# Casts of a projection's weights placed behind the sigmoids and evictions of the stage before, and two buffers for the latents

## The chip, the core and the metric

The kernel runs on one NeuronCore of a Trainium2 chip. Its engines work side by side, each through its own queue of instructions in order: TensorE (PE in the profile, with PEld for its weight loads), VectorE (DVE), ScalarE (ACT), GpSimd (POOL) and SyncE (SP), which here issues every DMA. An instruction that waits holds up all that stands behind it on its engine. The metric is the time of one execution on the device in microseconds (us), as the median of several runs.

## The reference, cut to what matters

A trunk of two layers over 512 tokens of width 1024. Layer 0 mixes with neighbourhood attention, layer 1 with latent attention; after each mixer comes a gated per-layer embedding.

```python
for i in range(DEPTH):
    xn = rmsnorm(x, norm_g[i])
    y = mixer_na(xn, ...) if i % 2 == 0 else mixer_mla(xn, ...)
    h = x + y
    gate = sigmoid(rmsnorm(h, ple_norm[i]) @ ple_w_gate[i])
    x = h + gate * (p[i] @ ple_w_proj[i])

# mixer_mla, its start:
c_q, c_kv, k_rope, z = split(xn @ w_in, [384, 640, 672], axis=-1)
q  = rmsnorm(c_q, q_norm) @ w_qb        # 16 heads of 64 + 32 (rotary)
kv = rmsnorm(c_kv, kv_norm) @ w_kvb
```

The change lies where layer 0 ends (its gate) and layer 1 begins: the projection to the latents `c_q`, `c_kv`, `k_rope` (672 columns), and the branch `z` (1024 columns).

## The kernel before

Tokens stand in four tiles of 128 rows (`t` = 0 to 3), and 1024 rows of weights in eight blocks `k`. A product of fp32 accuracy is made of three matmuls, high by high, low by high and high by low. Each weight matrix is therefore loaded raw and split by a cast: ACT writes the high part, DVE or POOL subtracts to get the low one. For the gate the parts are in fp32r (tiles `whi`, `wlo`, made by `load_w`); for layer 1's input projection in fp16 (tiles `whl`, and one `whx`), after a scaling by a power of two (`sc`) that depends on the sum of squares of the whole matrix.

**The end of layer 0, `gate_phase`.** The 1024 output columns go in two halves, `n` = 0 and 1; in each half four products of 24 matmuls, one for each `t`, go into two PSUM banks (`ps_mm`) in turn. A bank comes free when ACT has put its sigmoid (`sg`, line 692) into SBUF; DVE multiplies it with the embedding `pe` (line 693) and adds it to the residual `r` (line 695). After `n` = 1 of each `t`, `done` forms `x1n`, the normed input of layer 1 (square on ACT, a power on POOL, a product on DVE, lines 237 to 244), PE turns it in eight transposes, and ACT and DVE write it as fp16 parts `x1h`, `x1l` (lines 196, 197).

**The weights of the latents, `mla_ahead`.** They are prepared while the gate runs, in steps that `gate_phase` calls after given (`n`, `t`). `mla_c0` and `mla_c1` lie in two tiles `cr` (384 columns of `k` = 0..3 and 4..7, and two blocks of 288), `mla_c2` and `mla_c3` (three blocks of 288 each) in two of the three raw buffers `wraw`, through which the gate's own weights pass as well. ACT squares all of them (line 635); `over_rows` sums on PE; `scale` forms `sc` and its inverse `un`; four steps `cast` make the fp16 weights of the 384 columns (`c_cast`, lines 672 and 673, two halves of 384 elements a step). Steps `fetch` load the weights of `z`.

**The start of layer 1, `mla_c`.** Part 0 makes 384 columns for each `t`, part 1 the other 288. ACT evicts them (line 721) into tiles `c`. During part 0 the code casts the weights of part 1 (`whl`, `whl`, `whx`) and squares those of `z`; then `value_scale` (lines 203 to 218) loads the value weights `wv` and squares them. Last, for each `t`, the latents are normed into a tile `cn` (lines 237 to 244, 746 to 754), turned in six transposes and split into `cT` and into the rows `slab` of the rotary key, which SP moves to where the heads want them (line 191). There is one buffer for `cn`. `mla_heads` runs six products of the branch `z` (`NEARLY`, 24 matmuls each), then the rotary part, queries and keys of the first heads (line 784), two more products of `z`, and the heads.

**What sets the order.** The program is not written in the order that runs. A scheduler of the framework places the instructions of each engine by priority and by what its own model expects to be ready; `issue_after` (and `behind`, several of them) tells it to place what is inside no sooner than behind a given instruction. The built order is fixed; only semaphore waits decide the times. Tiles of a pool take over the place of a tile that has been released, and wait for its readers.

Of the kernel before, what the change touches and what calls it, by code (L numbers as in the profile page):

```python
# [14 lines left out]
F32 = mybir.dt.float32  # L15
# [4 lines left out]
AF = mybir.ActivationFunctionType  # L20
# [3 lines left out]
P = 128  # L24
S = 512
# [7 lines left out]
UP = 32768.0  # L33
# [12 lines left out]
class Trunk:  # L46
# [573 lines left out]
    def mla_ahead(self, junk, xinv):  # L620

        nc, a = self.nc, self.a
        raw = [self.big.tile([P, 1824], F32, name="cr", tag="big") for i in range(2)]
        raw += [self.wp.tile([P, 1024], F32, name="wraw", tag="wraw", bufs=3)[:, :864] for i in range(2)]
        ss = [self.small.tile([P, 8], F32, name="wss", tag="wss", bufs=4)[:, :4] for i in range(2)]
        self.c_raw, self.c_w, self.z_raw, self.z_sq = raw, [], [], []

        zj = [self.zp.tile([P, S], F32, name="z", tag="z") for i in range(2)]

        def load():  # L630
            for r, w in zip(raw, a["mla_c"]):
                nc.sync.dma_start(r, w)

        def square(r, c, k, i):
            nc.scalar.activation(junk[:, :c.stop - c.start], raw[r][:, c], AF.Square, accum_out=ss[k][:, i:i + 1])

        def squares(r):
            if r < 2:
                for i in range(2):
                    square(r, slice(768 * i, 768 * i + 768), 0, 2 * r + i)  # L640
                square(r, slice(1536, 1824), 1, r)
            else:
                square(r, slice(0, 864), 1, r)

        def scale():
            s = self.power(self.over_rows(ss), UP ** -2)
            u = self.small.tile([P, 8], F32, name="un", tag="un", bufs=8)[:, :2]
            nc.vector.reciprocal(u, s)
            nc.vector.tensor_scalar(u, u, xinv, None, op0=ALU.mult)
            self.c_scale = [(s[:, i:i + 1], u[:, i:i + 1]) for i in range(2)]  # L650

        def cast(q):
            h = self.pair16()
            self.c_cast(h, 0, raw[q // 2][:, q % 2 * 768:(q % 2 + 1) * 768], 0, 384)
            self.c_cast(h, 384, raw[q // 2][:, q % 2 * 768:(q % 2 + 1) * 768], 384, 384)
            self.c_w.append(h)

        def fetch(i):
            f, sq = self.fetch16([a["mla_z"][2 * i], a["mla_z"][2 * i + 1]], by="dve" if i in (2, 3) else "act",
                                 junk=zj[i // 2].bitcast(BF16))  # L660
            self.z_raw.append(f)
            self.z_sq += sq

        P_ = partial
        return {(0, 0): [load, P_(squares, 0)], (0, 1): [P_(squares, 1)], (0, 2): [P_(squares, 2), P_(squares, 3)],
                (0, 3): [scale], (1, 0): [P_(cast, 0), P_(cast, 1), P_(fetch, 0)], (1, 1): [P_(cast, 2), P_(cast, 3), P_(fetch, 1)],
                (1, 2): [P_(fetch, 2)], (1, 3): [P_(fetch, 3)]}

    def c_cast(self, h, o, r, c, w, part=0):
        nc = self.nc  # L670
# [4 lines left out]
    def gate_phase(self, pool, layer, hnT, rh, res, after, steps):  # L675
        nc, a = self.nc, self.a
        for n in range(2):
# [3 lines left out]
            for t in range(NT):  # L681
# [3 lines left out]
                w = S // 2 if last else S  # L685
                for o in range(0, S, w):
                    ps = self.psum("mm")[:, :w]
                    L = lambda s, k: hnT[t][:, s * KD + k, :]
                    W = lambda s, k: ws[k // 2][s][:, (k % 2) * S + o:(k % 2) * S + o + w]
                    self.mms(ps, self.by_chunk(L, W))  # L690
                    sg = pool.tile([P, S], F32, name="sg", tag="sg", bufs=2)[:, :w]
                    nc.scalar.activation(sg, ps, AF.Sigmoid, scale=rh[t])  # L692
                    nc.vector.tensor_tensor(out=sg, in0=pe[:, o:o + w], in1=sg, op=ALU.mult)  # L693
                    r = res[t][:, n * S + o:n * S + o + w]
                    nc.vector.tensor_tensor(out=r, in0=r, in1=sg, op=ALU.add)
                    after(t, n, o, w)
# [4 lines left out]
    def mla_c(self, pool, xT, cT, sets, xinv):  # L701
        nc, a = self.nc, self.a
# [9 lines left out]
        for part, (w0, wn) in enumerate(((0, 384), (384, 288))):  # L712
            un = self.c_scale[part][1]
            for t in range(NT):
# [3 lines left out]
                else:  # L718
                    W = lambda s, k: self.c_w[k // 2][:, s, (k % 2) * 384:(k % 2 + 1) * 384]
                self.mms(ps[:, :wn], self.by_chunk(lambda s, k: L(xT[s], k, t), W))  # L720
                nc.scalar.activation(cs[t][:, w0:w0 + wn], ps[:, :wn], AF.Copy, scale=un)
                if part == 0 and t < 3:
                    h = self.pair16() if t < 2 else pool.tile([P, 2, 1024], F16, name="whx", bufs=1)
                    if t == 0:
                        for i in range(2):
                            self.c_cast(h, 288 * i, self.c_raw[i], 1536, 288, 1)
                    else:
                        self.c_cast(h, 0, self.c_raw[1 + t], 0, 432, 1)
                        self.c_cast(h, 432, self.c_raw[1 + t], 432, 432, 1)
                    w1.append(h)  # L730
                if part == 0:
                    for i in range(2):
# [4 lines left out]
        slab_l = pool.tile([P, S], F32R, name="slab_l", tag="slab", bufs=2)  # L737
        for t in range(NT):
            c = cs[t]
            cn = pool.tile([P, 768], F32, name="cn", tag="cn", bufs=1)  # L740
            self.rms(cn[:, 0:384], c[:, 0:384], gq, 384)
            self.rms(cn[:, 384:640], c[:, 384:640], gkv, 256)
            cos, sin = tok[:, t, 0, :], tok[:, t, 1, :]
# [531 lines left out]
```

## Time and profile before

| | |
|---|---|
| median of 3 runs | 661.76 us (661.69 to 662.82) |
| the profiled execution: its own time | 659.6 us |
| its span, first to last instruction | 657.8 us |
| TensorE clock granted, mean of the span | 0.996 |
| matmuls | 3737 |
| moved by DMA | 80.2 MB, 122 GB/s on average |

The profiled execution is one run, 2.2 us under the median; its time holds 1.8 us outside the span. In what follows, columns of the table of windows are: the stretch and its length in us, then for each engine busy us and number of instructions, then the granted TensorE clock, the share of DMA engines busy, and GB/s. Rows of the timeline are: start, length (us), engine, line, operation, out<-in, shape, count; in brackets the idle time before it on that engine and what ended it.

### The profile page before, as it was taken

The numbers are of one execution on the slowest core, as the hardware profiler recorded it, in microseconds if no ns is written. First come the engines' busy times: TensorE is split into PE (matmuls) and PEld (weight loads), VectorE is DVE, ScalarE is ACT, GpSimd is POOL, SyncE is SP. The second block draws the span as 40 slices with busy tenths as digits, with TensorE's granted clock in tenths as the row PEclk, the third lists the DMA queues.
The fourth block names the chain that finished last, engine by engine and source line by source line (L and its number), as shares of the span: only waits on it lengthen the run. The fifth ranks groups of instructions, "written<-read, shape, count | busy, mean of one in ns | idle before, by whom it ended". The sixth has DMA issues, their size and how long they took to land.

```text
span 657.8 us, 10705 instructions
## 1 busy us (share of the span) xinstructions
PE 641.7 (98%) x3737; PEld 471.7 (72%) x3737; DVE 415.4 (63%) x955; ACT 435.3 (66%) x942; POOL 292.2 (44%) x295
## 2 busy tenths in 40 slices
PE   8999999999999999998999999999999999999995
PEld 6876575766856778886766454877777877788885
DVE  6387986867757316647767335888888874134543
ACT  6789977976757743655668445888878887245333
POOL 0341232342427575332102221686959776672721
PEclk9999999999999999999999999999999999999998
DMA  8957132400104055621860024120302222961122
GB/s 279 413 204 295 65 105 77 183 24 1 37 13 145 28 197 222 244 97 64 300 240 18 13 72 108 40 77 25 81 18 69 60 97 78 352 224 67 65 80 96
DMA packets 32327, 80.20 MB, mean 122 GB/s; under 512 B 4497, under 2 KB 9361, under 8 KB 32273
## 3 DMA queue, kind: packets, MB, share of 16 engines
q1 hardware_dynamic: 32272, 79.52, 34.4%
q8 instruction: 29, 0.48, 0.3%
q14 instruction: 26, 0.21, 0.1%
HBM read 67.97 MB, written 8.39 MB: 116 GB/s over the span
## 4 chain that ended last, share of the span: by engine, by line
PE 68%; ACT 11%; DVE 10%; DMA 4%; issue 4%; SPq 2%; POOL 1%; POOLq 0%; DVEq 0%; ACTq 0%
PE ps_mm L226 35%; PE ps_S L226 11%; PE ps_mm L784 5%; PE ps_T L255 5%; PE ps_T L226 3%; PE ps_O L226 2%; PE ps_O L898 2%; ACT whl L164 2%; DMA wraw<-gate 2%; PE ps_T L553 1%; PE ps_O L454 1%; ACT ex L878 1%; DMA wraw<-na_z 1%; ACT junk L137 1%; SPq L191 1%
## 5 line engine op out<-in xcount | busy, mean ns | idle before, releaser
L89 POOL TENSOR_TENSOR wlo<-wraw,whi 128x1024 fp32r<-128x1024 f32 (+3 forms) x63 | 109.5, 1759 | 67.0 <-ACT whi L88 34.0
L226 PEld LDWEIGHTS <-whl 128*128 128x128 f16 x648 | 62.3, 98 | 71.4 <-issue 1.3
L880 POOL TENSOR_TENSOR ex<-ex,rc 128x512 f32<-128x512 f32 x64 | 66.1, 1043 | 32.4 <-DVE rc L879 23.2
L88 ACT ACTIVATE whi<-wraw 128x1024 fp32r<-128x1024 f32 (+3 forms) x65 | 50.9, 812 | 43.0 <-DMA wraw<-gate 17.8
L226 PE MATMUL ps_mm<-whi,hnT 128*128 128x512 f32 (+1 forms) x272 | 70.2, 379 | 2.6 <-ACT sg L692 2.6
L226 PE MATMUL ps_mm<-xh,whl 128*128 128x512 f16 x304 | 72.6, 379 | 0.0
L197 DVE SCALAR_TENSOR_TENSOR pt<-ps_T,pt 128x512 f16<-128x512 f32 (+1 forms) x96 | 62.5, 661 | 15.6 <-ACT pt L196 15.3
L196 ACT ACTIVATE pt<-ps_T 128x512 f16<-128x512 f32 (+1 forms) x96 | 53.5, 575 | 9.3 <-PE ps_T L553 5.4
L226 PEld LDWEIGHTS ps_mm<-whi,hnT 128*128 128x128 f32 x272 | 49.2, 188 | 12.1 <-ACT sg L692 3.0
L540 POOL TENSOR_TENSOR ex<-ex,rc 128x128 f32<-128x128 f32 (+1 forms) x64 | 34.4, 569 | 50.5 <-DVE rc L536 42.2
L876 DVE TENSOR_REDUCE mx<-ps_S 128x1 f32<-128x512 f32 x64 | 43.7, 688 | 10.4 <-PE ps_S L226 9.1
L878 ACT ACTIVATE ex<-ps_S,mx 128x512 f32<-128x512 f32 x64 | 43.8, 685 | 9.7 <-DVE mx L876 8.8
L165 DVE SCALAR_TENSOR_TENSOR whl<-wr,sc,whl 128x512 f16<-128x512 f32 x64 | 45.6, 762 | 4.1 <-ACT whl L164 3.9
L239 POOL TENSOR_TENSOR rs<-ss,half 128x1 f32<-128x1 f32 x20 | 11.4, 576 | 76.3 <-DVE ss L238 76.2
L164 ACT ACTIVATE whl<-wr,sc 128x512 f16<-128x512 f32 x64 | 41.1, 712 | 4.4 <-DVE sc L100 2.6
L226 PE MATMUL ps_mm<-wlo,hnT 128*128 128x512 f32 (+1 forms) x136 | 40.6, 379 | 0.0
L255 PE MATMUL ps_T<-ident,ex 128*128 128x128 f32 x256 | 38.5, 273 | 0.0
L99 POOL TENSOR_TENSOR sc<-sc,half 128x1 f32<-128x1 f32 (+2 forms) x15 | 10.7, 713 | 62.2 <-DVE sc L98 62.2
L693 DVE TENSOR_TENSOR sg<-pe,sg 128x512 f32<-128x512 f32 (+1 forms) x17 | 21.6, 1270 | 24.7 <-ACT sg L692 24.7
L255 PEld LDWEIGHTS ps_T<-ident,ex 128*128 128x128 f32 x256 | 31.2, 140 | 8.2 <-POOL ex L880 1.1
L226 PE MATMUL ps_mm<-xl,whl 128*128 128x512 f16 x152 | 36.2, 379 | 0.0
L226 PE MATMUL ps_mm<-whl,xh 128*128 128x256 f16 x224 | 30.9, 273 | 0.6 <-DVE vt L197 0.3
(376 smaller groups left out, 1526.2 us busy)
## 6 DMA issues: line engine op xcount, KB each, us to landing
wr<-na_qk SPq DMA_DIRECT2D x16, 512.0 KB, 5.7
wraw<-gate SPq DMA_DIRECT2D x16, 512.0 KB, 3.3
pe<-pe SPq DMA_DIRECT2D x24, 256.0 KB, 7.0
wr<-na_v SPq DMA_DIRECT2D x8, 512.0 KB, 7.1
wraw<-na_o SPq DMA_DIRECT2D x8, 512.0 KB, 4.1
wr<-mla_z SPq DMA_DIRECT2D x8, 512.0 KB, 9.7
wraw<-mla_o SPq DMA_DIRECT2D x8, 512.0 KB, 4.9
wraw<-na_z SPq DMA_DIRECT2D x6, 512.0 KB, 7.8
```

What stands on the lines that cost most here:

```text
L88: nc.scalar.activation(hi[:, c], raw[:, c], AF.Copy)
L89: (rest or nc.gpsimd).tensor_tensor(out=lo[:, c], in0=raw[:, c], in1=hi[:, c].bitcast(F32), op=ALU.subtract)
L164: self.cast = [nc.scalar.activation(h[:, 0, c], r[:, c], AF.Copy, scale=s), nc.vector.scalar_tensor_tensor(h[:, 1, c], r[:, c], s, h[:, 0, ...
L165: nc.vector.scalar_tensor_tensor(h[:, 1, c], r[:, c], s, h[:, 0, c], op0=ALU.mult, op1=ALU.subtract)]
L196: self.last_split = nc.scalar.activation(hi, src, AF.Copy, scale=scale)
L197: nc.vector.scalar_tensor_tensor(lo, src, scale, hi, op0=ALU.mult, op1=ALU.subtract)
L226: last = self.last_mm = nc.tensor.matmul(out, l, r, start=i == 0, stop=i == n - 1)
L255: self.last_mm = self.nc.tensor.transpose(t[:, i * P:(i + 1) * P], b, self.ident)
L540: nc.gpsimd.tensor_tensor(out=e, in0=e, in1=rc[:, qt:qt + 1].to_broadcast([P, e.shape[1]]), op=ALU.mult)
L876: nc.vector.reduce_max(mx, sp, axis=AX.X, negate=True)
L878: nc.scalar.activation(ex, sp, AF.Exp, bias=mx, accum_out=sm)
L880: nc.gpsimd.tensor_tensor(out=ex, in0=ex, in1=rc.to_broadcast([P, S]), op=ALU.mult)
```

## The change

Four things are changed.

1. The four steps `cast` move: one after (1, 0), two after (1, 1), one after (1, 2), where two stood after (1, 0) and two after (1, 1); and each is placed behind the last sigmoid (`self.last_sg`). The casts for part 1 are placed behind the eviction of part 0 for the same `t`.
2. `mla_c2` and `mla_c3` are loaded in four pieces of 432 columns into buffers of the pool `zp`, which hold the branches' outputs `z`, instead of into two of the three `wraw`. Their squares and sums are six numbers in place of four.
3. The power in `scale` gets the priority that `scale16` has.
4. `cn` has two buffers.

```diff
-        raw += [self.wp.tile([P, 1024], F32, name="wraw", tag="wraw", bufs=3)[:, :864] for i in range(2)]
-        ss = [self.small.tile([P, 8], F32, name="wss", tag="wss", bufs=4)[:, :4] for i in range(2)]
+        raw += [self.zp.tile([P, S], F32, name="z", tag="z")[:, :432] for i in range(4)]
+        ss = [self.small.tile([P, 8], F32, name="wss", tag="wss", bufs=4)[:, :n] for n in (4, 6)]
...
-            for r, w in zip(raw, a["mla_c"]):
+            for r, w in zip(raw, a["mla_c"][:2] + [w[:, c:c + 432] for w in a["mla_c"][2:] for c in (0, 432)]):
                 nc.sync.dma_start(r, w)
...
-                square(r, slice(0, 864), 1, r)
+                square(r, slice(0, 432), 1, r)
...
         def scale():
-            s = self.power(self.over_rows(ss), UP ** -2)
+            ps = self.over_rows(ss)
+            with self.tc.high_priority(offset=300):
+                s = self.power(ps, UP ** -2)
...
         def cast(q):
             h = self.pair16()
-            self.c_cast(h, 0, raw[q // 2][:, q % 2 * 768:(q % 2 + 1) * 768], 0, 384)
-            self.c_cast(h, 384, raw[q // 2][:, q % 2 * 768:(q % 2 + 1) * 768], 384, 384)
+            with self.behind(self.last_sg):
+                for i in range(2):
+                    self.c_cast(h, 384 * i, raw[q // 2][:, q % 2 * 768:(q % 2 + 1) * 768], 384 * i, 384)
...
-        return {(0, 0): [load, P_(squares, 0)], (0, 1): [P_(squares, 1)], (0, 2): [P_(squares, 2), P_(squares, 3)],
-                (0, 3): [scale], (1, 0): [P_(cast, 0), P_(cast, 1), P_(fetch, 0)], (1, 1): [P_(cast, 2), P_(cast, 3), P_(fetch, 1)],
-                (1, 2): [P_(fetch, 2)], (1, 3): [P_(fetch, 3)]}
+        return {(0, 0): [load, P_(squares, 0)], (0, 1): [P_(squares, 1)], (0, 2): [P_(squares, 2 + i) for i in range(4)],
+                (0, 3): [scale], (1, 0): [P_(cast, 0), P_(fetch, 0)], (1, 1): [P_(cast, 1), P_(cast, 2), P_(fetch, 1)],
+                (1, 2): [P_(cast, 3), P_(fetch, 2)], (1, 3): [P_(fetch, 3)]}
...
-                    nc.scalar.activation(sg, ps, AF.Sigmoid, scale=rh[t])
+                    self.last_sg = nc.scalar.activation(sg, ps, AF.Sigmoid, scale=rh[t])
...
-                nc.scalar.activation(cs[t][:, w0:w0 + wn], ps[:, :wn], AF.Copy, scale=un)
+                ev = nc.scalar.activation(cs[t][:, w0:w0 + wn], ps[:, :wn], AF.Copy, scale=un)
                 if part == 0 and t < 3:
+                  with self.behind(ev):
...
-            cn = pool.tile([P, 768], F32, name="cn", tag="cn", bufs=1)
+            cn = pool.tile([P, 768], F32, name="cn", tag="cn", bufs=2)
```

Since the scheduler sets the order, three places of the built programs follow. The first is ACT in the second half of the gate, from the last sigmoid before the casts on (`sg` are the sigmoids, `whl<-cr` the casts, `x1n` the squares for the norm). Before:

```order
L692 ACTIVATE sg<-ps_mm,rs 128x512
L672 ACTIVATE whl<-cr,sc 128x384 x8
L672 ACTIVATE whl<-cr,sc 128x288 x2
L672 ACTIVATE whl<-wraw,sc 128x432 x2
L692 ACTIVATE sg<-ps_mm,rs 128x512 x2
L237 ACTIVATE x1n,ss<-r 128x1024 x2
```

In the changed program the same stretch of ACT reads:

```order
L695 ACTIVATE sg<-ps_mm,rs 128x512 x4
L675 ACTIVATE whl<-cr,sc 128x384 x2
L237 ACTIVATE x1n,ss<-r 128x1024
L695 ACTIVATE sg<-ps_mm,rs 128x512
L675 ACTIVATE whl<-cr,sc 128x384 x4
L237 ACTIVATE x1n,ss<-r 128x1024
L196 ACTIVATE x1h<-ps_T,sc 128x4x128 x2
L695 ACTIVATE sg<-ps_mm,rs 128x512
L675 ACTIVATE whl<-cr,sc 128x384 x2
```

Twelve casts stood in one piece ahead of the sigmoids of `t` = 0 and 1; now eight stand behind three of them, and the four of part 1 have gone to the stage after it, behind its evictions.

The second place is ACT at the end of the six early products of `z` (`z<-ps_mm` evicts one of them, `cT` and `slab_h` split the turned latents; the last `slab_h` belongs to `t` = 3; `ke` to `qo` evict the first heads' keys and queries, `rh` their rotary part). Before:

```order
L290 ACTIVATE z<-ps_mm,un 128x512
L88 ACTIVATE whi<-wraw 128x384 x2
L290 ACTIVATE z<-ps_mm,un 128x512
L176 ACTIVATE cT_3857<-ps_T 128x4x128
L176 ACTIVATE cT_3857<-ps_T 128x128
L176 ACTIVATE slab_h<-ps_T 128x128
L164 ACTIVATE whl<-wr_3849,sc 128x512 x4
L176 ACTIVATE ke_3863<-ps_S 64x512
L176 ACTIVATE ko_3865<-ps_S 64x512
L176 ACTIVATE qe_3859<-ps_S 64x512
L176 ACTIVATE qo_3861<-ps_S 64x512
L816 ACTIVATE rh<-ps_mm 128x512
```

And in the changed program:

```order
L176 ACTIVATE cT_3865<-ps_T 128x4x128
L176 ACTIVATE cT_3865<-ps_T 128x128
L176 ACTIVATE slab_h<-ps_T 128x128
L290 ACTIVATE z<-ps_mm,un 128x512
L88 ACTIVATE whi<-wraw 128x384 x2
L290 ACTIVATE z<-ps_mm,un 128x512
L164 ACTIVATE whl<-wr_3857,sc 128x512 x2
L820 ACTIVATE rh<-ps_mm 128x512
L164 ACTIVATE whl<-wr_3857,sc 128x512 x2
L176 ACTIVATE ke_3871<-ps_S 64x512
```

The last splits of the latents moved ahead of the last two evictions of `z`, and the eviction of the rotary part ahead of those of the keys and queries. On PE the six transposes of `t` = 3 stood behind all 144 matmuls of the six products; now 42 of these stand behind them.

The third place is SP from the last weights of `z` (`wr<-mla_z`) to the first move of `slab`. Before:

```order
L128 DMA wr_3849<-mla_z 128x1024 x2
L204 DMA wv<-mla_kv 128x4x512
L87 DMA wraw<-mla_qr 128x192 x2
L87 DMA wraw<-mla_kv 128x512
L1135 DMA spill_84<-r 128x1024
L87 DMA wraw<-mla_kv 128x512
L203 DMA gcol<-kv_norm 128x2x1
```

And in the changed program, from the same weights of `z` on:

```order
L128 DMA wr_3857<-mla_z 128x1024 x2
L87 DMA wraw<-mla_qr 128x192 x2
L87 DMA wraw<-mla_kv 128x512 x2
L87 DMA wraw<-mla_qn 128x384 x2
L1139 DMA spill_84<-r 128x1024
L203 DMA gcol<-kv_norm 128x2x1
L707 DMA tok<-rope_tok 128x128
L248 DMA gq<-q_norm 128x384
L248 DMA gkv<-kv_norm 128x256
L204 DMA wv<-mla_kv 128x4x512
L87 DMA wraw<-mla_qr 128x192 x2
```

The load of `wv` moved behind eleven other issues. In the changed program its tile takes the place of the first `cr`, and the issue waits for DVE's cast of the 288 columns from it, which is now in `mla_c`; before, it waited for PE alone.

More of the change, by code (lines that the diff above doesn't have):

```diff
@@ L727, in mla_c @@
                     else:
-                        self.c_cast(h, 0, self.c_raw[1 + t], 0, 432, 1)
-                        self.c_cast(h, 432, self.c_raw[1 + t], 432, 432, 1)
+                        for i in range(2):
+                            self.c_cast(h, 432 * i, self.c_raw[2 * t + i], 0, 432, 1)
                     w1.append(h)
```

## The prediction

> **What bounds the kernel.** I read the page's head first: TensorE is busy for 98% of the span, so a gain has to be idle time of PE.
>
> ```profile
> span 657.8 us, 10705 instructions
> PE 641.7 (98%) x3737; PEld 471.7 (72%) x3737; DVE 415.4 (63%) x955; ACT 435.3 (66%) x942; POOL 292.2 (44%) x295
> ```
>
> Second, the table of windows over the stages that the change touches (first column after the length: PE).
>
> ```profile
> 250.00:305.00 55.00, 55.00 (x267) 45.52 (x266) 32.76 (x38) 27.72 (x48) 22.70 (x13) 1.00 0.45 159
> 305.00:315.00 10.00, 7.45 (x33) 5.83 (x32) 9.60 (x21) 8.03 (x15) 0.59 (x1) 1.00 0.14 38
> 330.00:340.00 10.00, 10.00 (x70) 6.93 (x69) 8.64 (x13) 4.90 (x12) 0.55 (x1) 1.00 0.93 336
> 340.00:350.00 10.00, 9.85 (x81) 7.21 (x80) 2.64 (x10) 6.95 (x15) 1.25 (x3) 1.00 0.13 41
> 380.00:390.00 10.00, 9.39 (x50) 4.98 (x49) 3.04 (x14) 4.59 (x13) 2.55 (x5) 1.00 0.12 39
> 400.00:410.00 10.00, 8.62 (x38) 4.33 (x37) 4.40 (x8) 4.60 (x9) 1.15 (x2) 1.00 0.33 98
> 420.00:640.00 220.00, 219.62 (x1218) 173.29 (x1218) 144.10 (x272) 146.26 (x303) 149.66 (x122) 1.00 0.29 97
> ```
>
> PE lacks nothing up to 305, 2.55 us in the second half of the gate, 0.15 at 340 to 350 (I take that as staying), 0.61 at the end of the six early `z` products, 1.38 around the first score. From 420 to 640 it lacks 0.38 in 220 us, so whatever PE gains ahead of that passes to the end. Third, PE's timeline at these gaps, with the releaser in brackets.
>
> ```profile
> 287.80 1.07 PE L226 MATMUL ps_mm<-whi,hnT 128*128 128x512 f32 x4
> 298.89 1.17 PE L226 MATMUL ps_mm<-whi,hnT 128*128 128x512 f32 x4
> 312.60 1.19 PE L226 MATMUL ps_mm<-whi,hnT 128*128 128x512 f32 x4 [2.56 <-ACT sg L692]
> 314.10 1.07 PE L226 MATMUL ps_mm<-whi,hnT 128*128 128x512 f32 x4
> 315.46 1.07 PE L226 MATMUL ps_mm<-whi,hnT 128*128 128x512 f32 x4
> 348.65 0.28 PE L211 MATMUL ps_T<-half,vss 128*128 128x1 f32 x2
> 357.35 1.89 PE L226 MATMUL ps_mm<-x1l,whl 128*128 128x512 f16 x8
> 359.07 3.62 PE L226 MATMUL ps_mm<-x1h,whl 128*128 128x512 f16 x16
> 388.34 0.82 PE L255 MATMUL ps_T<-ident,cn 128*128 128x128 f32 x6
> 389.77 0.98 PE L784 MATMUL ps_mm<-cT,whi 128*128 128x512 f32 x3 [0.61 <-ACT cT L176]
> 401.51 1.89 PE L226 MATMUL ps_mm<-x1h,whl 128*128 128x512 f16 x8 [0.78 <-ACT z L290]
> 407.00 0.70 PE L226 MATMUL ps_S<-ke,qe 96*128 96x512 f32 x2
> 408.16 0.47 PE L226 MATMUL ps_S<-ke,qe 96*128 96x512 f32 x1 [0.45 <-DMA qe<-rl]
> ```
>
> Fourth, ACT's timeline ahead of the first gap.
>
> ```profile
> 285.28 1.06 ACT L88 ACTIVATE whi<-wraw 128x1024 fp32r<-128x1024 f32 x1 [0.37 <-DMA wraw<-gate]
> 286.25 0.67 ACT L692 ACTIVATE sg<-ps_mm,rs 128x512 f32<-128x512 f32 x1
> 305.87 5.01 ACT L672 ACTIVATE whl<-cr,sc 128x384 f16<-128x384 f32 x10 [3.63 <-DVE sc L100]
> 311.88 1.25 ACT L692 ACTIVATE sg<-ps_mm,rs 128x512 f32<-128x512 f32 x2
> ```
>
> **Part 1, casts behind sigmoids: −2.55.** The second half of the gate starts on PE at 298.89. From 314.10 to 315.46 six matmuls take 1.36, 0.227 each, so `t` = 0 is done 24 × 0.227 = 5.4 later, at 304.3. Its sigmoid comes only at 311.88, behind ten casts (row at 305.87) and two more that follow them; they waited for `sc` until 305.87 and took 6.0. PE wants that bank for `t` = 2 after 48 matmuls, at 309.8, and waits 2.56. In the new order of ACT no cast is ahead of the sigmoid of `t` = 0: it runs at 304.3 to 305.0, 4.8 before the bank is wanted, and that of `t` = 1 at 309.8 is wanted at 315.2. At most two casts, 1.0 us, stand ahead of it. The gap goes; the bound is 0 to 2.55.
>
> What is late next are the casts and splits themselves, now between the norms. The chain from the sigmoid of `t` = 0 to its norm's end took from 311.88 to 317.53, the end of the first row below: 5.65. Further rows are the sums of squares of `z`'s weights, and two groups of DVE from 300 to 350 (total, and mean in ns).
>
> ```profile
> 316.25 1.28 DVE L244 SCALAR_TENSOR_TENSOR x1n<-r,rs,gn 128x1024 f32<-128x1024 f32 x1 [0.66 <-POOL rs L239]
> 334.06 1.22 DVE L133 CUSTOM_DVE_ANT_0 z<-wr 128x1024 bf16<-128x1024 f32 x1
> ...
> L693 DVE TENSOR_TENSOR sg<-pe,sg 128x512 f32<-128x512 f32 x5 | 5.5, 1100 | 3.0 <-ACT sg L692 3.0
> L695 DVE TENSOR_TENSOR r<-r,sg 128x512 f32<-128x512 f32 x5 | 3.5, 691 | 0.1
> L197 DVE SCALAR_TENSOR_TENSOR x1l<-ps_T,sc,x1h 128x512 f16<-128x512 f32 x8 | 5.8, 747 | 3.0 <-ACT x1h L196 3.0
> ```
>
> From 304.3 that gives 309.9, or 310.9 with two casts on ACT ahead; the built order of PE places these transposes after some 70 of the half's 96 matmuls, at 298.9 + 70 × 0.227 = 314.8. Slack 3.9. The tightest is the low part of `t` = 3 on DVE. From the end of that sigmoid, about 325.6, DVE has its product and sum, four sums of squares, a norm, and four low parts: 1.10 + 0.69 + 4 × 1.22 + 1.28 + 4 × 0.75 = 10.9, all done at 336.5, the first of `t` = 3 at 335.8. PE gets to them at about 336.5: slack 0.7. Then the casts for part 1, now between evictions: they end on DVE near 341, and PE, which finishes part 0 near 340, wants the first there and the last, `whx`, near 343. I take 0 for all, with up to 2.0 as the upper bound if the order has a place that this misses.
>
> Moving the squares costs too. The first sigmoid of the first half stands behind one more `whi` (1.06, row at 285.28); it ended at 286.92, would end at 287.0 to 288.0 as three short waits ahead of it go, and PE wanted that bank at 287.80 (row above). I take 0, bound 0.2. Six numbers in place of four add two reads of the accumulator and two short instructions, some 0.1 us each on ACT, beside a PE that runs on other banks: 0. The four raw pieces are issued early, into buffers that nothing uses, and free the third `wraw` for the gate: 0, or a gain that PE can't show, as it has no idle time before 305. The power's priority makes `sc` earlier, which shortens nothing once the casts are no longer ahead: 0.
>
> **Part 2, two buffers for `cn`: −0.61 −0.78 −0.60.** With one buffer, the next `cn` starts only when PE has turned the last one.
>
> ```profile
> 366.33 0.09 DVE L746 MEMSET cn<- 128x32 f32 x1 [4.61 <-PE ps_T L255]
> 369.40 0.48 DVE L244 SCALAR_TENSOR_TENSOR cn<-c,rs,gkv 128x256 f32<-128x256 f32 x1
> 402.15 0.69 DVE L818 TENSOR_TENSOR rh<-ps_mm,rope_c 128x512 f32<-128x512 f32 x1 [1.08 <-DMA rope_c<-rope_c]
> ```
>
> From the start of one to its end at 369.88 are 3.6 us. With two it is made ahead, and the scheduler has moved the transposes: 42 matmuls of `z` stand behind the last six, at (359.07 − 357.35) / 8 = 0.215 each, 9.0 us. The wait of 0.61 for the split `cT` after them is covered by these 9.0. If it does not go, it costs 0.61.
>
> Behind the same `cT` and `slab` stands SP: twelve moves, then the rotary table.
>
> ```profile
> 391.48 0.60 SPq L191 DMA_DIRECT2D ke<-slab_h  x1
> 399.13 0.59 SPq L773 DMA_DIRECT2D rope_c<-rope_c  x1
> ```
>
> `rope_c` is issued at 399.13 and DVE gets it at 402.15, 3.0 later; ACT's eviction of the next `z` is behind the rotary part in ACT's queue and PE's last `z` product waits 0.78 for it; the rest of the 1.38 of that window, 0.60, goes at the first scores, 0.45 of it for `qe`, which is moved from the rotated `rl`. In the new order the last transposes end at 389.16 − 2.55 − 9.0 = 377.6; the first move followed them by 2.3, so 379.9; 7.65 for twelve moves brings `rope_c` to 387.6 and its landing to 390.6. PE reaches the rotary product at 389.16 − 2.55 = 386.6, and ACT evicts it ahead of the keys and queries instead of behind them. DVE's 402.15 becomes about 391, and with the 5 to 6 us that follow it `qe` lands at 397, before the first score at 407.00 − 2.55 − 0.61 − 0.78 − 0.15 (0.60 − 0.45) = 402.9. All three waits go; if `rope_c` were held as before, 1.38 stay. Bounds of part 2: 0 to 1.99.
>
> The other side of it: transposes placed earlier can wait for `cn`. In the built order the pieces for `t` = 1, 2 and 3 start some 0.2, 7.8 and 13.2 us behind those of `t` = 0; with a chain of 3.6 each, two tiles ahead, I find at least 2.8 us of slack. I take 0.
>
> **Part 3, `wv` later: 0.** Its load now waits for DVE's cast of the first 288 columns, which stands right behind the last low part (336.5 by the count above, so about 337.3), and is issued behind eleven other issues. It lands d later. The first rows give KB and median us to landing.
>
> ```profile
> cr<-mla_c SPq DMA_DIRECT2D x2, 912.0 KB, 4.7
> wv<-mla_kv SPq DMA_DIRECT2D x1, 1024.0 KB, 11.4
> 344.94 1.14 ACT L208 ACTIVATE wv<-wv,gcol 128x1024 f32<-128x1024 f32 x1
> ```
>
> Its own 11.4 was taken when the DMA share was 0.93 (330 to 340); from 340 on it is 0.13. Nearest in size is `cr`; scaled by its size, 1024 KB takes 4.7 × 1024 / 912 = 5.3. Two squares follow, 2.3 us, and PE wants their sums at 348.65 − 2.55 = 346.1. So PE stands still for d − 6.5: nothing at 5.3, with 1.2 to spare, and 4.9 at 11.4. I take 0, bounds 0 to 4.9. Queued behind the waiting issue on SP stand pieces of the heads' weights, which PE first reads in the row of 389.77: no cost. Queued behind PE's sum stand the rest of part 1 and all products of `z`.
>
> The Trainium skill, "DMA: Bandwidth & Descriptors", section "Anatomy of one DMA — SWDGE (gpsimd) path", gives about 2.0 us plus bytes over 436 GB/s: an estimate of 4.4 us for `wv`, near the 5.3 taken. By it the row of 4.7 for 912 KB would be 4.1, and its own row of 11.4 disagrees; with either of the lower numbers the sum stays.
>
> **Sum.** 2.55 + 0.61 + 0.78 + 0.60 = 4.54: the profiled execution's span goes from 657.8 to 653.3, its time from 659.6 to 655.1. The median stands 2.2 above that execution, so I take the difference from it: 661.76 − 4.5 = **657.3 us**.
>
> **Rivals.** *`wv` comes late (slower).* The load takes 11.4 as before, and the cast that releases it comes 2 us later than my count, at 339.3: squares end at 353.0, PE stalls 6.9: 661.76 − 4.54 + 6.9 = 664.1. It decides for slower by over 0.2% (663.1) once the landing is past 349.7, a stall of 5.9; landing at 348.7, with only the 11.4, gives 662.1. For it: the only row of this transfer, and a DVE busy 8.64 of 10 ahead of the release. Against: `z`'s weights are fetched earlier now, the eleven issues ahead hold small pieces, and all other rows are shorter. The Trainium skill, "TensorE: Matmul & The Clock Gate", Part 1, says that PE idle for a window of some 3.4 us drops to half clock; a stall of 4.9 would then, as an estimate from that figure, cost up to 1.7 us more in the next window. The gap of 2.56 left the granted clock at 1.00 in its window, and no run here shows a longer one in mid-kernel.
>
> *The `z` stage gives nothing*, because transposes that moved ahead wait for `cn` as much as they saved: 661.76 − 2.55 = 659.2. For it: the chain of 3.6 is longer than the 2.0 to be won. Against: the slack of 2.8.
>
> *The first gap comes back* in the gate or the latents, as a cast or split ahead of what PE waits for (the 0.7 of `t` = 3): 661.76 − 1.99 = 659.8. For it: DVE is busy 9.60 of 10 at 305 to 315 and has the same work to do.
>
> *Nothing happens*: both of these together, 661.8.
>
> **How the numbers follow.** All gains, within 1 us of the sum (656.3 to 658.5): 0.65. One of the two halves (658.5 to 660.4): 0.20. Nothing, within 0.2% of before, about what a measurement of this kernel can tell from no change (660.4 to 663.1): 0.09. `wv` late, beyond: 0.06. So faster 0.85, same 0.09, slower 0.06. The range leaves out the last two, and at the lower end goes 1.4 below the sum, as the 2.2 between execution and median may come out otherwise: 655.9 to 660.4.
>
> **What would show it.** In the profile after: no wait of PE for `sg` behind the gate's line 226; sigmoids of the second half at about 304, 310, 315 and 321, casts behind them; `slab` moves from 380 and `rope_c` from 388; the last `z` product and the first score, near 403, without idle time; `wv` issued near 337 and landed by 343, with the product of `half` and `vss` unwaited. Wrong it would be if PE idles at `ident,cn`, `ident,x1n` or `half,vss`.

## The result, and the profile after

| | us |
|---|---|
| before, median in the same measurement | 662.27 (661.69 to 662.82) |
| changed kernel, three of its four runs | 654.02, 654.15, 654.85 |
| ratio | 0.988, 95% interval 0.9861 to 0.990 |
| predicted | 657.3 (655.9 to 660.4) |

The change gives 8 us, in the direction that was forecast, but nearly twice the 4.5 of the sum, and below the range. The profiled execution of that measurement took 1683.7 us, with matmuls more than twice as long (834 ns in the mean for 512 columns of fp16, where e2 has 379), so the profile after is that of a repeat of the same kernel (653.96 us; experiment e2). First the head of its page, then its table of windows, in the columns of before.

```profile
span 652.2 us, 10714 instructions
PE 639.7 (98%) x3739; PEld 471.6 (72%) x3739; DVE 409.4 (63%) x955; ACT 435.9 (67%) x946; POOL 291.4 (45%) x295
```

```profile
305.00:315.00 10.00, 10.00 (x46) 8.27 (x45) 7.26 (x13) 6.44 (x12) 0.99 (x2) 1.00 0.76 253
380.00:390.00 10.00, 10.00 (x47) 6.03 (x46) 1.40 (x4) 4.35 (x8) 1.98 (x2) 1.00 0.64 176
400.00:410.00 10.00, 10.00 (x51) 7.70 (x49) 4.47 (x10) 6.52 (x13) 4.27 (x5) 1.00 0.20 52
420.00:640.00 220.00, 219.66 (x1220) 173.56 (x1219) 141.86 (x266) 143.59 (x296) 146.02 (x120) 1.00 0.29 98
```

The idle time of 2.55, 0.61 and 1.38 us is gone; behind 420 the same 0.34 to 0.38 is left. PE's timeline at the places of the three gaps:

```profile
298.84 0.40 PE L112 MATMUL ps_T<-ssb,ones 128*128 128x1 bf16 x10
309.62 0.62 PE L226 MATMUL ps_mm<-wlo,hnT 128*128 128x512 f32 x2
310.08 1.07 PE L226 MATMUL ps_mm<-whi,hnT 128*128 128x512 f32 x4
346.00 0.28 PE L211 MATMUL ps_T<-half,vss 128*128 128x1 f32 x2
376.49 0.82 PE L255 MATMUL ps_T<-ident,cn 128*128 128x128 f32 x6
386.02 1.73 PE L788 MATMUL ps_mm<-cT,whi 128*128 128x512 f32 x6
401.86 1.04 PE L226 MATMUL ps_S<-ke,qe 96*128 96x512 f32 x3
402.73 1.09 PE L788 MATMUL ps_mm<-cT,whi 128*128 128x512 f32 x4
```

No row has a wait. The last transposes of `cn` stand at 376.49 and the first product with `cT` at 386.02; 42 products of `z` lie between. The places that were forecast, on the queue of SP:

```profile
337.19 0.38 SPq L204 DMA_DIRECT2D wv<-mla_kv  x1
378.98 0.61 SPq L191 DMA_DIRECT2D ke<-slab_h  x1
386.62 0.58 SPq L777 DMA_DIRECT2D rope_c<-rope_c  x1
```

`wv` is issued at 337.19 (forecast 337.3), the first move of `slab` at 378.98 (379.9), `rope_c` at 386.62 (387.6). So the mechanism went as written, and 3.5 us more came from somewhere.

To find where, I cut every profile at three marks of PE: the product for the weights' sums (`ssb,ones`, the start of the gate's second half), the product for `wv` (`half,vss`), and the product with `cT` behind the first three scores. Of before, with 348.65 shown with the prediction, the first and the last are:

```profile
298.68 0.35 PE L112 MATMUL ps_T<-ssb,ones 128*128 128x1 bf16 x8
408.47 1.09 PE L784 MATMUL ps_mm<-cT,whi 128*128 128x512 f32 x4
```

The stages are differences of such starts; "rest" is the span less the last mark, "gap" the longest wait of PE for a sigmoid in the gate's second half.

| kernel | up to the sums | gate and latents | gap in it | `z` to the scores | rest |
|---|---|---|---|---|---|
| before, first profile | 298.68 | 49.97 | 2.56 | 59.82 | 249.33 |
| before, e1 | 298.50 | 52.70 | 3.24 | 59.78 | 249.22 |
| changed, e2 | 298.84 | 47.16 | none | 56.73 | 249.47 |
| one `cn`, e3 | 299.20 | 47.16 | none | 59.74 | 249.50 |
| casts moved alone, e4 | 299.08 | 47.11 | none | 59.65 | 249.36 |
| part 1's casts alone, e5 | 300.77 | 50.45 | 1.29 | 59.55 | 249.43 |
| longer gap, e6 | 300.28 | 55.04 | 4.75 | 59.71 | 249.27 |
| two `cn` alone, e7 | 300.37 | 53.75 | 3.23 | 56.87 | 249.31 |
| casts back, e8 | 301.13 | 47.17 | none | 56.75 | 249.45 |
| no priority, e10 | 298.57 | 47.16 | none | 56.71 | 249.46 |
| changed, e11 | 298.64 | 47.16 | none | 56.74 | 249.46 |
| casts back, e12 | 299.03 | 47.17 | none | 56.72 | 249.48 |
| raw tiles alone, e13 | 299.97 | 47.17 | none | 59.61 | 249.45 |

Each stage has its price: some 3.0 us in the `z` stage for the second buffer, in every pair; and in the gate 2.8 to 7.9 us over 47.16 for the gap. That is 0.25 more than a gap of 2.56, but 2.3 to 3.4 more than the gaps over 3 us. (The 3.29 of e5 hold a second wait, told below.)

### The profile page after: what moved, and what is told of

Same layout as the page of the kernel before. It is cut to its first block, busy times and chain, and to the rows that moved or that the text cites. A ratio compares the mean times of both kernels' runs of the same rounds, so it can differ in the third digit from the quotient of the medians.

```text
span 1681.9 us, 10714 instructions
## 1 busy us (share of the span) xinstructions
PE 1672.9 (99%) x3739; PEld 892.2 (53%) x3739; DVE 411.3 (24%) x955; ACT 449.7 (27%) x946; POOL 291.5 (17%) x295
## 4 chain that ended last, share of the span: by engine, by line
PE 99%; issue 0%; DVE 0%; ACT 0%; POOL 0%; POOLq 0%; DVEq 0%; ACTq 0%
PE ps_mm L226 52%; PE ps_S L226 14%; PE ps_T L255 7%; PE ps_mm L788 7%; PE ps_T L226 3%; PE ps_O L902 3%; PE ps_O L226 3%; PE ps_mm L301 3%; PE ps_T L553 2%; PE ps_O L454 1%; PE ps_S L517 1%; PE ps_S L518 1%; PE ps_S L788 1%; PE ps_T L1015 0%; PE ps_T L551 0%
## 5 line engine op out<-in xcount | busy, mean ns | idle before, releaser
L226 PEld LDWEIGHTS <-whl 128*128 128x128 f16 x648 | 111.2, 174 | 252.6 <-issue 245.7
L226 PE MATMUL ps_mm<-xh,whl 128*128 128x512 f16 x304 | 190.6, 834 | 0.0
L226 PE MATMUL ps_mm<-whi,hnT 128*128 128x512 f32 (+1 forms) x272 | 169.0, 799 | 0.0
L226 PE MATMUL ps_mm<-xl,whl 128*128 128x512 f16 x152 | 95.4, 836 | 0.0
L226 PE MATMUL ps_mm<-wlo,hnT 128*128 128x512 f32 (+1 forms) x136 | 92.9, 791 | 0.0
L255 PE MATMUL ps_T<-ident,ex 128*128 128x128 f32 x256 | 92.3, 537 | 0.0
L226 PE MATMUL ps_mm<-x1h,whl 128*128 128x512 f16 x128 | 79.3, 833 | 0.0
L226 PE MATMUL ps_S<-ke,qe 96*128 96x512 f32 x96 | 70.8, 890 | 0.0
L226 PE MATMUL ps_S<-ko,qo 128*128 128x512 f32 x96 | 69.1, 854 | 0.0
L788 PE MATMUL ps_mm<-cT,whi 128*128 128x512 f32 x94 | 64.6, 840 | 0.0
```

The source lines that it names most:

```text
L226: last = self.last_mm = nc.tensor.matmul(out, l, r, start=i == 0, stop=i == n - 1)
L255: self.last_mm = self.nc.tensor.transpose(t[:, i * P:(i + 1) * P], b, self.ident)
L788: self.last_mm = nc.tensor.matmul(PS[key], *terms[i], start=i == 0, stop=i == len(terms) - 1)
```

## The experiments

**e1, before again.** No edit.

> The kernel before, unchanged, for a second profile. The first measurement gave a gain of 7.8 us where 4.5 was forecast, and the profiled execution of before (659.6) is 2.2 us under its timed ones. Theory A (the terms were sized right, the rest is a part of the change that was costed at nothing): the profile again shows PE idle of 2.55, 0.61 and 1.38 us at the three places, span within 0.5 us of 657.8. Theory B (the profiled execution is not the usual one, and usual ones hold 2 us more idle time that the change removes too): span near 660, with an idle time of PE of about 2 us that the first profile does not have.

661.65 us, median of ten runs (659.93 to 664.9); profile 660.2. PE's timeline there has this at the gap, and the windows the clock (the column behind POOL):

```profile
304.75 1.49 PE L226 MATMUL ps_mm<-wlo,hnT 128*128 128x512 f32 x4
306.08 1.08 PE L226 MATMUL ps_mm<-whi,hnT 128*128 128x512 f32 x4
309.72 0.61 PE L226 MATMUL ps_mm<-wlo,hnT 128*128 128x512 f32 x2
313.57 2.05 PE L226 MATMUL ps_mm<-whi,hnT 128*128 128x512 f32 x4 [3.24 <-ACT sg L692]
315.42 1.05 PE L226 MATMUL ps_mm<-wlo,hnT 128*128 128x512 f32 x2
316.27 1.45 PE L226 MATMUL ps_mm<-whi,hnT 128*128 128x512 f32 x4
317.56 0.62 PE L226 MATMUL ps_mm<-wlo,hnT 128*128 128x512 f32 x2
```

```profile
305.00:315.00 10.00, 6.62 (x26) 4.82 (x25) 9.64 (x19) 7.25 (x14) 1.56 (x2) 0.93 0.08 28
315.00:330.00 15.00, 15.00 (x75) 11.94 (x74) 9.41 (x15) 8.22 (x15) 1.64 (x3) 0.93 0.89 329
```

The gap is 3.24 instead of 2.56, and the first four matmuls behind it take 1.85 instead of 0.91: half speed. The ten from 313.57 to 317.56 take 3.99 where ten of 0.227 take 2.27, so 1.72 are lost while PE counts as busy. With the gap and 0.42 at 304.75 (four matmuls in 1.33) that is 5.4 of the 5.54 over the changed kernel. The windows' 0.93 agree: half clock for 1.4 of the first 10 us and for 2.1 of the next 15, some 3.5 in all. Theory B holds, in a form that it did not name: not more idle time alone, but slow matmuls behind it. In this measurement's 28 runs of before, ten have a mean clock of 0.996 or more, with a median of 660.4 us; eighteen have 0.994 or less, with a median of 663.3; the gate stages of the two profiles differ by 2.7. (In the later measurements the two groups are less clear: some runs of before at 0.996 took 662 to 663 us.)

The Trainium skill, "TensorE: Matmul & The Clock Gate", Part 1, gives an idle window of about 3.4 us as what sends PE to half clock, and says that this window runs freely. The traces agree only in part: gaps of 1.29 (e5) and 2.56 did not, 3.23 (e7), 3.24 and 4.75 (e6) did, so that less than 3.4 us of idle time was enough; e7 shows that 2.0 us were.

**e2, the changed kernel again.** No edit.

> The changed kernel, unchanged, for a profile of one of its usual executions, since the profiled one took 1683.7 us. Expected 654.2 us, span 652.4; no idle time of PE behind the sigmoids, none at the last products of z and the first score. Theory A: some 3.4 us of PE time are gone at a fourth place, seen against the first profile. Theory B: only 4.5 us less idle than in the first profile of before, and the rest is the difference between the two profiles of before.

654.0 us (ratio 0.9877, 0.9845 to 0.9909); the profile shown above.

**e3, one buffer for `cn`, all else changed.**

```diff
-            cn = pool.tile([P, 768], F32, name="cn", tag="cn", bufs=2)
+            cn = pool.tile([P, 768], F32, name="cn", tag="cn", bufs=1)
```

> The changed kernel with one buffer for the latents again, nothing else undone. By the forecast's terms it gives back 2.0 us: 656.2, with PE idle again some 0.6 us before the first product with cT and 1.4 around the first score. Rival, that the z stage gave nothing: 654.2, the same as the changed kernel. Rival, that the z stage gave the missing 3.4 as well: 659.5.

657.8 us (0.9934, 0.9913 to 0.9954), 3.8 above the changed kernel by the medians, 3.4 between the two profiles: 3.0 of it in the `z` stage, 0.4 ahead of the sums. Its PE timeline has the old waits back:

```profile
387.34 0.96 PE L788 MATMUL ps_mm<-cT,whi 128*128 128x512 f32 x3 [0.61 <-ACT cT L176]
399.05 1.89 PE L226 MATMUL ps_mm<-x1h,whl 128*128 128x512 f16 x8 [0.78 <-ACT z L290]
405.79 0.47 PE L226 MATMUL ps_S<-ke,qe 96*128 96x512 f32 x1 [0.56 <-DMA qe<-rl]
```

The waits alone sum to 2.0 as forecast, the starts to 3.0. The figure in brackets counts from the end of the last matmul, but a matmul that does not wait starts before that end. In the first profile of before, six transposes of 0.11 from 388.34 end their slots at 389.00, and the product with `cT` comes at 389.77: 0.77 lost for a wait of 0.61. Likewise 0.93 for the 0.78 (398.85 + 8 × 0.216 to 401.51). At the scores, 3.51 pass from the last eight matmuls of `z` to the next product with `cT` in before (to 408.47), and 2.41 in e2 (to 402.73), so 1.10 for the 0.60 (first row before, second row e2):

```profile
404.96 1.89 PE L226 MATMUL ps_mm<-x1h,whl 128*128 128x512 f16 x8
400.32 1.89 PE L226 MATMUL ps_mm<-x1h,whl 128*128 128x512 f16 x8
```

That is 2.80 of the 3.09 between these two profiles; the expectation of e7 below counts 1.26 at the scores, which these rows do not give.

**e4, only the casts moved, on the kernel before.** These lines of the change, with `last_sg` and `ev` set as there:

```diff
+            with self.behind(self.last_sg):
...
-                (0, 3): [scale], (1, 0): [P_(cast, 0), P_(cast, 1), P_(fetch, 0)], (1, 1): [P_(cast, 2), P_(cast, 3), P_(fetch, 1)],
-                (1, 2): [P_(fetch, 2)], (1, 3): [P_(fetch, 3)]}
+                (0, 3): [scale], (1, 0): [P_(cast, 0), P_(fetch, 0)], (1, 1): [P_(cast, 1), P_(cast, 2), P_(fetch, 1)],
+                (1, 2): [P_(cast, 3), P_(fetch, 2)], (1, 3): [P_(fetch, 3)]}
...
+                  with self.behind(ev):
```

> The kernel before with only the casts moved behind the sigmoids and the evictions; raw tiles in wraw, one buffer for the latents. By the forecast's terms minus 2.55: 659.5 against 662.1 for before. Rival, that the raw tiles in z matter (the gate's own weights wait for wraw when the casts come later): above 661.

657.68 us (0.9927, 0.9904 to 0.9951): minus 5 instead of 2.55, and not slower for the raw tiles in `wraw`, as the rival had it. No gap, no run with a clock under 0.997.

**e5, only part 1's casts moved.**

```diff
+                ev = nc.scalar.activation(cs[t][:, w0:w0 + wn], ps[:, :wn], AF.Copy, scale=un)
                 if part == 0 and t < 3:
+                  with self.behind(ev):
```

> The kernel before with only the four casts of part 1 moved behind the evictions; eight casts still stand ahead of the sigmoids, so the gap in the gate should shrink by 2.2 us to about 1. Theory C (idle time, and above it a drop of the clock that a gap of 3.2 us or more sets off): no run with a mean clock under 0.996, time about 658.5, that is 2.2 us under the quick runs of before (660.0 to 660.9) and 4 under its median of 662.8. Theory I (idle time alone, the clock has another cause): 2.2 us under the median of before, 660.6, with runs at a clock of 0.992 to 0.994 among them as in before.

659.94 us (0.9974, 0.9954 to 0.9995). The gap is 1.29, and eleven of twelve runs have a clock of 0.996 or more; one has 0.995, which theory C did not allow, but none has the 0.992 to 0.994 of theory I. The time is 1.4 above the 658.5 of theory C. The profile (662.0, one of the slower of the twelve) has a wait that no other kernel has:

```profile
313.92 1.20 PE L226 MATMUL ps_mm<-whi,hnT 128*128 128x512 f32 x4 [1.29 <-ACT sg L692]
341.75 0.50 PE L226 MATMUL ps_S<-whl,x1l 128*128 128x384 f16 x2 [1.06 <-DVE x1l L197]
```

With the eight casts still in one piece and part 1's behind them, a low part `x1l` is late, behind three sums of squares of `z`'s weights on DVE; the prediction had seen 0.7 us of slack at the low parts of `t` = 3 in the full change.

**e6, a longer gap.** Four casts are made twice, with the same values; three of the copies stand ahead of the first sigmoid.

```diff
-        nc.scalar.activation(h[:, 0, o:o + w], r[:, c:c + w], AF.Copy, scale=s)
+        for _ in range(2 if w == 384 and o else 1):
+            nc.scalar.activation(h[:, 0, o:o + w], r[:, c:c + w], AF.Copy, scale=s)
```

> The kernel before with four of the eight casts of the 384 columns made twice on ACT (the second writes the same values), three of them ahead of the first sigmoid of the second half: the gap grows by 1.5 us, to 4 or more. Theory C: every run has the drop, none with a mean clock above 0.994, and the profile shows half speed behind the gap; time 664 to 666, 1.5 above the slow runs of before. Theory I: all runs 1.5 us later, 664.3 in the median, with quick ones near 661.9 at a clock of 0.996 among them.

664.27 us (1.0025, 1.0 to 1.005); all twelve runs at a clock of 0.991 to 0.994. Of PE's timeline, and of the windows:

```profile
316.56 2.07 PE L226 MATMUL ps_mm<-whi,hnT 128*128 128x512 f32 x4 [4.75 <-ACT sg L693]
320.99 1.05 PE L226 MATMUL ps_mm<-wlo,hnT 128*128 128x512 f32 x2
321.85 1.34 PE L226 MATMUL ps_mm<-whi,hnT 128*128 128x512 f32 x4
```

```profile
315.00:320.00 5.00, 3.44 (x8) 2.76 (x9) 4.83 (x10) 3.90 (x8) 0.06 (x1) 0.56 0.26 64
320.00:330.00 10.00, 10.00 (x45) 8.18 (x44) 4.01 (x5) 1.87 (x4) 1.04 (x2) 0.88 0.97 354
```

Two matmuls still take 0.86 at 320.99, 4.4 us behind the gap, so half speed lasted longer than in e1: from 315.6 to 322.4 by the windows (4.4 of the first 5 us, 2.4 of the next 10). The stage is 7.88 above the changed kernel's for a gap of 4.75. Theory C holds in its main point: lengthen the gap and the drop is there in every run; shorten it (e5) or close it (e4) and no run shows a clock of 0.994 or less. That it takes a gap of 3.2 us is not shown, as e7 tells.

**e7, only the second buffer.**

```diff
-            cn = pool.tile([P, 768], F32, name="cn", tag="cn", bufs=1)
+            cn = pool.tile([P, 768], F32, name="cn", tag="cn", bufs=2)
```

> The kernel before with only the second buffer for the latents. By the forecast's terms minus 2.0: 660.8 against a median of 662.8, still in two groups of runs as before. By start-to-start times (each stop of PE costs its idle time and some 0.16 us more, as the first matmul behind it does not overlap the one before): 0.77 + 0.93 + 1.26 = 2.96, so 659.8. Rival, that the second buffer brings 3.8, as the undoing of it in the changed kernel cost: 659.0.

659.79 us against 662.4, by the medians minus 2.6; the ratio (0.9941, 0.9913 to 0.9968) leaves 2.1 to 5.8 open, so the time does not decide between 2.96 and the 3.8 of the rival. The stage does: 56.87 against 59.8, some 2.9. The runs are in two groups as before (656.3 to 658.0 at 0.996 or more, 658.8 to 662.1 below). Its gap of 3.23 has the drop too, and at a higher price than in e1:

```profile
311.59 0.61 PE L226 MATMUL ps_mm<-wlo,hnT 128*128 128x512 f32 x2
315.43 2.07 PE L226 MATMUL ps_mm<-whi,hnT 128*128 128x512 f32 x4 [3.23 <-ACT sg L692]
```

```profile
310.00:315.00 5.00, 2.20 (x10) 1.50 (x8) 5.00 (x10) 5.00 (x11) 0.00 (x0) 0.92 0.00 0
315.00:320.00 5.00, 4.57 (x11) 3.60 (x12) 4.27 (x8) 3.25 (x6) 0.55 (x1) 0.50 0.46 107
320.00:330.00 10.00, 10.00 (x50) 8.30 (x49) 4.49 (x7) 3.00 (x6) 0.55 (x1) 0.95 1.01 378
```

A mean clock of 0.92 over 5 us is half clock for 0.8 of them: the clock fell near 314.2, only 2.0 us after PE's last matmul (311.59 + 0.61), and came back near 321. So the length of a gap alone does not decide; the 2.56 of the first profile of before was longer than these 2.0. The trace's record of the clock has the stretch of half clock as 3.41 us in e1 and as 6.83 in e6 and e7, once and twice the same time. In each of the three, the drop in the gate and the one behind the last matmul of the program lie 100 or 101 times 3.413 us apart. If the clock is decided at such points only, a gap counts by how it lies to them: in the first profile of before, 652.45 (the drop at its end) less 100 × 3.413 is 311.1, which cuts its gap (310.05 to 312.60) into 1.1 and 1.5 us. That is an estimate from these four traces; no run moved a gap of one length to test it.

**e8 and e12, the casts back at their old places.** All else is changed as in the change.

```diff
-            with self.behind(self.last_sg):
...
-                (0, 3): [scale], (1, 0): [P_(cast, 0), P_(fetch, 0)], (1, 1): [P_(cast, 1), P_(cast, 2), P_(fetch, 1)],
-                (1, 2): [P_(cast, 3), P_(fetch, 2)], (1, 3): [P_(fetch, 3)]}
+                (0, 3): [scale], (1, 0): [P_(cast, 0), P_(cast, 1), P_(fetch, 0)], (1, 1): [P_(cast, 2), P_(cast, 3), P_(fetch, 1)],
+                (1, 2): [P_(fetch, 2)], (1, 3): [P_(fetch, 3)]}
...
-                  with self.behind(ev):
```

> The changed kernel with the casts back at their old places (two steps after (1, 0), two after (1, 1), nothing placed behind sigmoids or evictions); raw tiles in z's buffers, priority of the power and two buffers of cn stay. Theory C: the gap in the gate is back, 2.6 us or more, with runs in two groups: 656.8 where the clock holds, 659 to 660 where it drops. If the earlier scale (priority) shortens the gap below 2.5: one group, near 656.

655.2 us (0.9871, 0.9827 to 0.9915), with no gap in the gate's second half though twelve casts stand ahead of its sigmoids again. The main case of the expectation did not come. An earlier scale did, but not by the priority (e10). The change's first part is not needed for the gain it was forecast to bring. Then beside the changed kernel on the same chip:

> The changed kernel with the casts at their old places, again, on the same chip as the changed one. Theory F: the two stages take 47.2 and 56.8 us as in the changed kernel, and the times agree within 0.5 us; what differed (655.2 against 654.0) came ahead of the gate's second half, where the profile had a wait of 1.4 us for the first sigmoid. Theory G: 1 us or more slower.

654.4 us (0.9877, 0.9864 to 0.989) against 654.09 in e11; from the sums' product on, every stage agrees to 0.02 us.

**e9 and e13, only the raw tiles moved into `z`'s buffers.** On the kernel before, with the loads, squares and casts in four pieces as in the change:

```diff
-        raw += [self.wp.tile([P, 1024], F32, name="wraw", tag="wraw", bufs=3)[:, :864] for i in range(2)]
-        ss = [self.small.tile([P, 8], F32, name="wss", tag="wss", bufs=4)[:, :4] for i in range(2)]
+        raw += [self.zp.tile([P, S], F32, name="z", tag="z")[:, :432] for i in range(4)]
+        ss = [self.small.tile([P, 8], F32, name="wss", tag="wss", bufs=4)[:, :n] for n in (4, 6)]
```

> The kernel before with only the raw tiles of mla_c2 and mla_c3 moved into z's buffers (six sums); casts at their old places, one buffer for the latents, no priority. Theory F (the gap of the gate came from the scale, late because POOL's power stood behind low parts of the gate's weights, which waited for raw buffers that mla_c2 and mla_c3 held): sc ready near 302 instead of 305.7, no gap in the gate, from the first product for the sums to that for wv 47.2 us instead of 50 to 53, time about 657.5, all clocks 0.996 or above. Theory G (the twelve casts ahead of the sigmoids are the cause as such): gap of 2.6 or more stays, 661 to 663.

659.0 us (0.9938, 0.9922 to 0.9955), clocks 0.996 to 0.998: in time between the two theories, and without a usable profile the cause stayed open. So the kernel ran again.

> The kernel before with only the raw tiles in z's buffers, again for a profile of a usual execution (the first one's took 1325 us throughout) . Theory F: no gap of PE in the gate's second half, scale ready within 4 us of the sums' product instead of 7, gate and latents 47.2 us, z stage 59.7 as in all kernels with one buffer for the latents; the time, 659 in the last job where 657.5 was expected, is then longer ahead of the gate's second half. Theory G: a gap of 1 to 2.5 us is left in the gate, below what the clock reacts to.

657.96 us (0.9945, 0.9924 to 0.9967), gate and latents 47.17. Before, the queues of POOL, DVE and ACT read:

```profile
302.08 2.40 POOL L89 TENSOR_TENSOR wlo<-wraw,whi 128x1024 fp32r<-128x1024 f32 x1 [4.77 <-ACT whi L88]
304.44 1.15 POOL L99 TENSOR_TENSOR sc<-sc,half 128x2 f32<-128x2 f32 x1
...
302.27 2.76 DVE L693 TENSOR_TENSOR sg<-pe,sg 128x512 f32<-128x512 f32 x1 [3.04 <-ACT sg L692]
305.67 0.16 DVE L100 TENSOR_SCALAR sc<-sc 128x2 int32<-128x2 int32 x1
...
300.60 1.06 ACT L88 ACTIVATE whi<-wraw 128x1024 fp32r<-128x1024 f32 x1 [5.25 <-DMA wraw<-gate]
```

And in e13:

```profile
281.05 9.48 POOL L89 TENSOR_TENSOR wlo<-wraw,whi 128x1024 fp32r<-128x1024 f32 x4
300.65 0.70 POOL L99 TENSOR_TENSOR sc<-sc,half 128x2 f32<-128x2 f32 x1 [10.12 <-DVE sc L98]
...
301.74 5.02 ACT L674 ACTIVATE whl<-cr,sc 128x384 f16<-128x384 f32 x10 [0.84 <-DVE sc L100]
306.66 1.19 ACT L674 ACTIVATE whl<-z,sc 128x432 f16<-128x432 f32 x2
307.76 0.67 ACT L694 ACTIVATE sg<-ps_mm,rs 128x512 f32<-128x512 f32 x1
```

The order on POOL is the same: four low parts of the gate's weights, then the power of the scale. Before, the fourth weight waited for its load, as `mla_c2` and `mla_c3` held two of three raw buffers (SP issued it at 297.34, when the third low part had ended; in e13 at 283.48); its low part ended at 304.48 and the power at 305.59. The same weight held the scale up on a second queue: ACT's sigmoid stood behind its cast, and DVE's next step for the scale (line 100, at 305.67) behind that sigmoid's product, which took 2.76 beside POOL's low part, where 0.69 is usual (e13 at 300.94). With all three buffers the low parts end at 290.5, and the power comes with its own input, at 300.65. The twelve casts then end 7.9 us behind the sums' product instead of 13.3 (311.98 less 298.68), and the sigmoid behind them frees its bank at 308.4, 2.6 us ahead of PE's need, which comes 11.1 us behind the sums' product (48 matmuls of 0.227 and the small products; 299.97 here). Theory F holds for the gap. Its time of 657.5 was missed by 0.5 (e13) and 1.5 (e9); in e13, 1.1 to 1.3 us more than in e2 and before pass ahead of the sums.

**e10, without the priority, and e11, the changed kernel beside it.**

```diff
-            with self.tc.high_priority(offset=300):
-                s = self.power(ps, UP ** -2)
+            s = self.power(ps, UP ** -2)
```

> The changed kernel without the priority of the power. The queue of POOL is the same, the scale comes at the same time: 0 within 0.5 us of the changed kernel's 654. Rival: the DVE steps of the scale come later, and the casts with them; still hidden unless by over 4 us.

> The changed kernel, unchanged, beside the two kernels that undo a part of it: 654.0, 47.2 us from the sums' product to that for wv and 56.8 from there to the first scores.

654.26 (0.9879, 0.9864 to 0.9894) and 654.09 us (0.9873, 0.9859 to 0.9887). The priority is worth nothing, as forecast. It does not even make the scale earlier: with it and without, the power starts 0.68 us behind the sums' product (299.32 less 298.64, and 299.25 less 298.57).

No version beats the changed kernel. One with fewer edits, the casts left where they were (e12), equals it.

## Why the prediction missed

**"I take the difference from it" is the step that failed first.** The profiled execution of before stood 2.2 us under the median, and the sum took those 2.2 as an offset of every kernel. They were mostly the price of the gap in the usual execution, and the change removes that too: in e1 the gap is 3.24 us long instead of 2.56, with half speed behind it. The gate's term, 2.55, was right as a bracket of one execution; the stage cost 2.81 there, 5.54 in e1, 6.59 in e7. The rule of the clock stood in the prediction, but only beside the rival of a late `wv`, where there was no stall. The gap of 2.56 had left the clock at 1.00 in one execution, and the sum priced it so for all. The spread of the three runs of before could not show that.

**"0.61 + 0.78 + 0.60" for the second buffer was mis-sized**: 3.0, not 1.99, most of the difference because each bracket leaves out the overlap that a stop loses (e3). Mechanism and places were right, to about 1 us.

**"The four raw pieces ... 0, or a gain that PE can't show" was wrong**, and "the gap goes" by the casts was half of the story. Moving the raw tiles closes the gap by itself (e13), moving the casts closes it by itself (e4), and both together bring no more (e12 against e11; e3, 657.8, against e4, 657.68). The prediction read ACT's wait for `sc` and did not follow it to POOL and DVE, where the scale stood behind work on a weight that had had no raw buffer. The sum was not hurt, since the gap was counted once.

**Right**: `wv` at nothing. The list of DMA issues of e2 has it at 5.1 us (5.3 taken, 11.4 feared), and PE's product of 346.00 has no wait. The 4.4 us that the prediction works out from the Trainium skill, "DMA: Bandwidth & Descriptors", section "Anatomy of one DMA — SWDGE (gpsimd) path", were 0.7 short; that section is on transfers issued from GpSimd, and SyncE issues `wv`.

```profile
wv<-mla_kv SPq DMA_DIRECT2D x1, 1024.0 KB, 5.1
```

Right too were the transposes moved ahead of `cn`, which wait for nothing, and the low parts of `t` = 3, counted to end at 336.5 and done at 336.49 in e2. That count has some luck in it: it starts from a sigmoid that ends at 325.6, where the signs put it at 321; it ran from 322.96 to 323.65. The priority was rightly priced at nothing for a wrong reason, an earlier scale. None of the rivals came.

The account against the first profile of before, 657.8 − 652.2 = 5.6: 2.81 in the gate, 3.09 in the `z` stage, less 0.16 ahead of the sums and 0.14 behind the scores. Against e1, a usual execution, 660.2 − 652.2 = 8.0: 5.54 in the gate, 3.05 in the `z` stage, less 0.34 ahead of the sums and 0.25 behind the scores.

**Open**: why the start of the gate's second half lies between 298.5 and 301.1 us from profile to profile, and so how much of the spread of before comes from there rather than from the clock. A part is on record: e8 has a wait of 1.38 us for the first sigmoid of the first half, e2 and e11 none; and in e7 the matmuls at the kernel's start go at half speed until 10.5 us, in the first profile of before until 7.3. With a longer wait for a first weight (0.63 against 0.29) that puts e7 1.4 us behind after a hundred matmuls (28.91 against 27.47; e5 has 28.81).

## What to carry to other kernels

Price a stop of TensorE from start to start, not by its idle bracket, and read the granted clock behind it in more than one profile: a stop of 2.6 to 3.2 us cost 2.8, 5.5 or 6.6 us here, and one profile may show the cheap kind. When a value is late, follow it through every queue it passes (here a power on POOL behind a weight that waited for a buffer): two edits that look like parts of one cure may each be the whole of it.

## What the runs showed of the hardware

Gaps of PE of 1.29 (e5) and 2.56 us (before) left the granted clock at 1.00. Gaps of 3.23 (e7), 3.24 (e1) and 4.75 us (e6) were followed by matmuls of 0.43 to 0.46 instead of 0.227 us. Half clock lasted 3.41 us in e1 (1.72 lost) and 6.83 us in e6 and e7. In e7 the clock fell 2.0 us after PE stopped, so a gap under 3 us is not safe by its length alone.

The mean clock of a run shows the drop as 0.991 to 0.994, against 0.996 to 0.998 for the kernels without a gap, where it falls only behind the last matmul (in the first profile of before from 652.45 us on). Runs of before at 0.996 can't be told apart by it.

A product on DVE took 2.76 us while POOL made a low part (before, 302.27), and 0.69 without (e13, 300.94).
